# Grouped-query attention on one core: rounds of six jobs instead of five, and a new order of work in each sort of job

## The chip, the core and the metric

The kernel runs on one NeuronCore of one Trainium2 chip. The engines are TensorE (PE; its weight loads are shown apart as PEld), VectorE (DVE), ScalarE (ACT), GpSimd (POOL) and SyncE (SP, which here only issues DMAs). The metric is the device time of one execution in microseconds (us), and the times of several executions are given by their median.

## The reference

Attention with 8 batches, 512 positions, 32 query heads, 8 key heads and 64 numbers a head; four query heads share one key head. All in float32:

```python
    scale = 1.0 / np.sqrt(dim)
    K_expanded = np.repeat(K, heads_per_group, axis=2)      # V likewise
    ...
    scores = np.einsum('bhqd,bhkd->bhqk', Q, K_expanded) * scale
    weights = np.exp(scores - np.max(scores, axis=-1, keepdims=True))
    weights = weights / (np.sum(weights, axis=-1, keepdims=True) + 1e-10)
    output = np.einsum('bhqk,bhkd->bhqd', weights, V_expanded)
```

## The kernel before

The work is cut into 64 jobs. A job is one key head of one batch with its four query heads, that is two pairs of heads (i = 0 and 1), and for each pair 4 key chunks (kc) times 2 heads (m): 16 blocks of 128 keys by 512 queries. Two jobs are a unit u, whose result `o_sb` is stored at once; eight jobs are a batch. Scores are computed transposed (keys on partitions), so that the exponentials can serve as weights of the second matrix product.

For each job:

- PE multiplies keys and queries (`scores`, line 280). Two blocks fill a tile `s_ps` of two banks of PSUM; there are two such tiles.
- ACT takes the exponential of a tile and writes float16 into `pt` (`act_tile`, line 296). A full tile is called a wide tile here, a single block a half tile.
- Two or three of the blocks of pair 1 don't go to ACT. DVE and POOL compute their exponentials by the bits of a float16: DVE turns scores into an integer `u` (`exp_d`, line 306, from the tile `d_ps`, of which there is one), masks its mantissa `f` (`exp_d2`, line 320), POOL computes `g` and the product `w`, and DVE adds `u` and `w` into `pt` (`exp_d4`, line 346). A job with three such blocks is called wide (`WIDE`, line 41), one with two narrow. Where a wide job is followed by a narrow one, DVE also computes `g`, so that POOL has `w` alone.
- PE multiplies `pt` and V (`pv`, line 365; 32 steps a pair, in an order of blocks that `blocks` gives). V has a column of ones, so the sums of the weights come along. There is one tile `pv` of PSUM for this.
- DVE takes the reciprocal of the sums and multiplies (`norm`, line 402) into `o_sb`.
- PE transposes the queries of the job after the next into a bank of `d_ps` (`trans_q`, line 207), and DVE copies them out to `qt`.

All of it is one long program whose order is written out by hand; every engine runs its instructions in that order and waits where it has to. The jobs overlap by one: in the loop's pass j, scores and exponentials are job j's, while `pv`, `norm` and `exp_d4` are those of `last`, job j − 1. A tile of a pool can be written anew when its last reader is done, so `pv` of a pair waits for the multiplication in `norm` of the pair before.

In the kernel before, jobs 4 to 61 are wide unless j % 5 is 2: four wide and a narrow one, from job 3 on. ACT runs a wide job's seven instructions as four wide tiles, a half tile and two wide tiles; the half tile's scores lie in a bank of `d_ps` beside the transposed queries. The third block of job j + 1 is multiplied and converted in job j, in the same bank, after ACT has read the half tile:

```python
        bank = d_tile()
        beside = act_tile(j, 4, bank) if taken(j) > 2 else None
        ...
        if taken(j + 1) > 2:
            exp_d(j + 1, 2, taken(j + 1), bank[:, 1:2, :], copies[0])()
```

`LOADS`, `KEYS` and `CHECKS` say in which job K, Q and V are loaded (on POOL's queue, ahead of the job's other work on POOL), in which SP's queue transposes a batch's keys (four transposing DMAs and two copies, `dma_k`), and in which DVE checks a quarter of a batch's V (`check_v`) and the sums of 16 pairs (`check_sums`); these checks decide at the end whether a general path has to run.

Of the kernel before, what the change touches and what calls it, by code (L numbers as in the profile page):

```python
# [40 lines left out]
WIDE = lambda j: 4 <= j < 62 and j % 5 != 2  # L41
# [26 lines left out]
def fast_path(ctx, tc, Q, K, V, out, flag, ident):  # L68
# [28 lines left out]
    ok = const_pool.tile([128, SPB * 2 * SC], FP32, name="ok")  # L97
    okv = const_pool.tile([128, B * SC], FP32, name="okv")
    okall = const_pool.tile([128, 1], FP32, name="okall")
# [152 lines left out]
    def act_tiles(j):  # L252
# [8 lines left out]
    CHECKS = {  # L261
        (j, at): divmod(n, SC) for n, (j, at) in enumerate(
            [(j, 0) for j in (3, 4, 6, 7, 8, 11, 12, 16, 17, 21, 22, 23, 26, 27, 31, 32)]
            + [(j, 0) for j in (36, 37, 38, 41, 42, 46, 47, 48, 51, 52, 56, 57, 60, 61, 62)]
            + [(62, 1)]
        )
    }

    KEYS = dict(zip((4, 10, 16, 26, 36, 41, 50), range(1, B)))
# [26 lines left out]
    def act_tile(j, n, spare=None):  # L296
        group = act_tiles(j)[n]
        i, kc, lo = group[0]
        ps = s_pool.tile([128, 2, S], FP32, name="s_ps") if spare is None else spare
        for _, _, m in group:  # L300
            scores(j, ps[:, m, :], i, kc, m)
        return nc.scalar.activation(  # L302
            out=jobs[j]["pt"][:, i, kc, lo:, :], in_=ps[:, lo:, :], func=EXP, scale=scale
        )

    def exp_d(j, lo, hi, ps, other=None):
        st = jobs.setdefault(j, {})
        if "u" not in st:
            for name, dtype in (("u", I16), ("f", I16), ("g", BF16), ("w", BF16)):
                st[name] = dve_pool.tile([128, 3, S], dtype, name=name + "16")[:, 0:taken(j), :]  # L310
        for n in range(lo, hi):
            apart(scores(j, ps[:, n - lo, :], DPAIR, *divmod(d_block(j) + n, 2)), other)
        return lambda: nc.vector.tensor_scalar(  # L313
            out=st["u"][:, lo:hi, :], in0=ps[:, 0:hi - lo, :], scalar1=A_U, scalar2=B_U,
            op0=ALU.mult, op1=ALU.add,
        )

    def exp_d2(j, engine=None):  # L320
        st = jobs[j]
        by_bits = engine is None
        engine = engine or nc.gpsimd
        odd = j == NJOB - 2 or WIDE(j) and not WIDE(j + 1)
        nc.vector.tensor_single_scalar(  # L325
            out=st["f"], in_=st["u"], scalar=1023, op=ALU.bitwise_and
        )

        def factor():
            (nc.vector if odd else engine).tensor_scalar(  # L330
                out=st["g"], in0=st["f"], scalar1=-EXP_F1,
                scalar2=EXP_K * 2.0 ** (24 * by_bits), op0=ALU.add, op1=ALU.mult,
            )

        def product():
            engine.tensor_tensor(  # L336
                out=st["w"], in0=st["g"], in1=st["f"].bitcast(FP16) if by_bits else st["f"],
                op=ALU.mult,
            )
# [18 lines left out]
    def blocks(j, i):  # L358
        if j == NJOB - 1:
            kcs = (0, 1, 3, 2)  # L360
# [24 lines left out]
    def in_bounds(outs, inv, first):  # L385
        ops = ((1.0 / SUM_HI, ALU.is_ge), (1.0 / SUM_LO, ALU.is_le))
        for out_, in1, (bound, op) in zip(outs, (first, outs[0]), ops):
            nc.vector.scalar_tensor_tensor(
                out=out_, in0=inv, scalar=bound, in1=in1, op0=op, op1=ALU.mult
            )  # L390


    full = []

    def check_sums():
        while full:
            flat = invs.pop(full.pop()).rearrange("p s m qc -> p (s m qc)")
            in_bounds((ok, ok), flat, ok)
# [3 lines left out]
    def norm(j, i):  # L402
# [15 lines left out]
        if left == 1:  # L418
            last_rights(LAST_SUMS - 4 * SC, LAST_SUMS, nc.vector)
            last_check()  # L420
        h = g * HPG + 2 * i
# [12 lines left out]
        if left > NLAST and n == SPB - 1:  # L434
            full.append(k)

    def all_checks():
        assert not full and not invs
        vmax = const_pool.tile([128, 1], FP32, name="vmax")
        nc.vector.tensor_reduce(out=vmax, in_=okv, op=ALU.max, axis=AX.X)  # L440
        okmin = const_pool.tile([128, 1], FP32, name="okmin")
        nc.vector.tensor_reduce(out=okmin, in_=ok, op=ALU.min, axis=AX.X)
        nc.gpsimd.tensor_scalar(
            out=okall, in0=vmax, scalar1=V_HI, scalar2=okmin, op0=ALU.is_le, op1=ALU.mult
        )

    LIMITS = ((1.0 / SUM_HI, ALU.is_ge), (1.0 / SUM_LO, ALU.is_le))
    rights = [const_pool.tile([128, LAST_SUMS], BF16, name=f"right{n}") for n in range(2)]

    def last_rights(lo, hi, first=None):  # L450
        inv = inv_last.rearrange("p s m qc -> p (s m qc)")
        for engine, right, (bound, op) in zip((first or nc.gpsimd, nc.gpsimd), rights, LIMITS):
            engine.tensor_scalar(
                out=right[:, lo:hi], in0=inv[:, lo:hi],
                scalar1=bound, scalar2=okall, op0=op, op1=ALU.mult,
# [48 lines left out]
    nc.gpsimd.memset(ok, 1.0)  # L504
# [53 lines left out]
    exp_d(0, 0, 2, d_tile())()  # L558
# [11 lines left out]
    for j in range(1, NJOB - 1):  # L570
        last = j - 1
        u, g = divmod(j, 2)
        b, gp = divmod(u, GP)
        open_job(j)
# [9 lines left out]
        cut = (11, 19) if taken(j) < 3 else (4, 18) if taken(last) < 3 else (4, 16)  # L584
        act_tile(j, 0)
        if j == 1:
            piece(1, *first_k(1, 0, bank[:, 1, S // 2:]))
        exp_d(j, 0, 2, d_tile())()
        act_tile(j, 1)
        if j % 5 == 3:  # L590
            check_sums()
        if (j, 0) in CHECKS:
            check_v(*CHECKS[j, 0])
        pv(last, 0, 0, 16)
        act_tile(j, 2)
        pv(last, 0, 16, 32)
        norm(last, 0)
        act_tile(j, 3)

        reads = []  # L600
        bank = d_tile()
        beside = act_tile(j, 4, bank) if taken(j) > 2 else None

        ahead = (j + 1,) if j < 2 else (3, 4) if j == 2 else (j + 2,)
        for n, to in enumerate(ahead):
            if to < NJOB:
                reads.append(trans_q(to, bank[:, n, :], other=beside)[1])
        if j == 1:
            reads.append(first_k(1, 1, bank[:, 1, :])[1])
        exp_d4(last)  # L610
        rest = exp_d2(j)
        copies = [read() for read in reads]
        if rest:
            rest()
        if taken(j) == 2:
            act_tile(j, 4)
        pv(last, 1, 0, cut[0])
        act_tile(j, 5)
        if beside:
            pv(last, 1, *cut)  # L620
        if taken(j + 1) > 2:
            exp_d(j + 1, 2, taken(j + 1), bank[:, 1:2, :], copies[0])()
        if (j, 1) in CHECKS:
            check_v(*CHECKS[j, 1])
        if not beside:
            pv(last, 1, *cut)
        act_tile(j, 6)
        pv(last, 1, cut[1], 32)
        norm(last, 1)
# [5 lines left out]
    exp_d(j, 0, 2, d_tile())()  # L635
# [140 lines left out]
```

## Time and profile before

| | |
|---|---|
| runs, median (lowest to highest) | 404.34 us (404.28 to 404.49), 3 runs |
| profiled execution, its own time | 404.57 us |
| its span, first to last instruction | 402.8 us |
| granted TensorE clock, mean | 0.999 |
| HBM read, written | 50.33 MB, 33.55 MB |

A row of a timeline has the start in us from the span's start, the length, engine, line, operation, what is written from what, shapes and count; rows of equal instructions that follow each other are merged, and in square brackets stands the idle time before and what ended it. A row of groups has count, busy us, mean ns of one, idle us before it. A row of landings has the number of DMAs, their size and the median us from issue to landing.

### The profile page before, as it was taken

The page shows a single profiled execution, that of the slowest core. Times are in us where ns is not written, and L with a number is a line of the kernel's source. Part 1 is how long each engine was busy: PE and PEld are TensorE (multiplying, and loading weights), DVE is VectorE, ACT ScalarE, POOL GpSimd, SP SyncE. Part 2 cuts the span into 40 slices and gives each one's busy share as a digit, 9 for nine tenths or more (in the row PEclk, how much of TensorE's full clock was granted, in tenths as well). Part 3 has the DMA queues.
Part 4 walks back from the last instruction along what each step waited for, and adds up shares of the span by engine and source line. Part 5 has one row for each costly group of instructions (what it writes and reads, how often), then busy time and mean ns, then how long its engine had stood idle before and what let it go on. Part 6 is the DMA issues. An engine that isn't in the chain of part 4 may idle for free.

```text
span 402.8 us, 12997 instructions
## 1 busy us (share of the span) xinstructions
PE 375.8 (93%) x5670; PEld 228.0 (57%) x5670; DVE 366.4 (91%) x635; ACT 393.9 (98%) x454; POOL 286.8 (71%) x169
## 2 busy tenths in 40 slices
PE   7999999999999999999999999999999999999985
PEld 3565555555555555555555555555555555556554
DVE  4788998999999999999999999999999999999996
ACT  5999999999999999999999999999999999999995
POOL 9848577597587687687687686677776767765752
PEclk9999999999999999999999999999999999999999
DMA  9979999899999259999259999679369959222206
GB/s 145 163 190 182 91 288 225 164 211 237 184 214 206 107 88 247 192 239 182 107 84 226 168 227 197 208 109 252 110 170 202 175 169 128 107 106 106 88 34 201
DMA packets 82893, 67.73 MB, mean 168 GB/s; under 512 B 52752, under 2 KB 57872, under 8 KB 82832
## 3 DMA queue, kind: packets, MB, share of 16 engines
q0 software_dynamic: 45072, 24.91, 48.3%
q1 hardware_dynamic: 36688, 41.49, 36.6%
q8 instruction: 45, 0.74, 0.7%
q10 hardware_dynamic: 1072, 0.46, 0.4%
q14 instruction: 16, 0.13, 0.1%
HBM read 50.33 MB, written 33.55 MB: 208 GB/s over the span
## 4 chain that ended last, share of the span: by engine, by line
ACT 29%; PE 25%; POOL 24%; DVE 20%; issue 2%; ACTq 0%; DVEq 0%
ACT pt L302 28%; POOL w L336 16%; PE pv L377 12%; PE s_ps L284 9%; POOL g L330 8%; DVE pt L349 8%; DVE o_sb L422 4%; DVE f L325 4%; DVE qt L220 2%; PE d_ps L215 2%; DVE g L330 1%; DVE inv L417 1%; PE d_ps L284 1%; PE s_ps L510 1%; PE d_ps L377 0%
## 5 line engine op out<-in xcount | busy, mean ns | idle before, releaser
L302 ACT ACTIVATE pt<-s_ps 128x1024 f16<-128x1024 f32 x400 | 379.0, 1122 | 0.3 <-PE s_ps L284 0.2
L336 POOL TENSOR_TENSOR w<-g,f 128x1536 bf16<-128x1536 bf16 (+1 forms) x63 | 179.6, 2851 | 37.6 <-DVE g L330 33.4
L377 PEld LDWEIGHTS <-pt 128*128 128x128 f16 x4096 | 142.1, 98 | 81.2 <-issue 41.6
L377 PE MATMUL pv<-v,pt 128*128 128x65 bf16 x4032 | 177.8, 195 | 3.7 <-DVE o_sb L422 2.2
L284 PE MATMUL s_ps<-qt,kt 64*128 64x512 bf16 x746 | 152.3, 384 | 12.0 <-ACT pt L302 10.0
L330 POOL TENSOR_SCALAR g<-f 128x1536 bf16<-128x1536 int16 (+1 forms) x50 | 67.1, 1341 | 69.1 <-DVE f L325 69.0
L313 DVE TENSOR_SCALAR u<-d_ps 128x1024 int16<-128x1024 f32 (+1 forms) x111 | 109.9, 990 | 0.3
L284 PEld LDWEIGHTS <-kt 64*128 64x128 bf16 x960 | 50.2, 93 | 55.3 <-issue 31.5
L422 DVE TENSOR_TENSOR o_sb<-pv,inv 128x512 f32<-128x512 f32 x112 | 77.5, 692 | 3.9
L284 PE MATMUL d_ps<-qt,kt 64*128 64x512 bf16 x214 | 58.4, 376 | 3.5 <-ACT pt L302 0.3
L349 DVE TENSOR_TENSOR pt<-u,w 128x1536 uint16<-128x1536 int16 (+1 forms) x64 | 56.4, 882 | 2.3 <-POOL w L336 0.2
L220 DVE COPY qt<-d_ps 128x1024 bf16<-128x1024 bf16 x62 | 42.3, 684 | 0.0
L215 PEld LDWEIGHTS <-q_nat 128*128 128x128 bf16 x508 | 28.5, 98 | 23.8 <-issue 23.8
L417 DVE RECIPROCAL inv<-pv 128x8 f32<-128x8 f32 x112 | 23.1, 207 | 17.4 <-PE pv L377 16.0
L215 PE MATMUL d_ps<-ident,q_nat 128*128 128x128 bf16 x496 | 38.3, 220 | 0.0
L302 ACT ACTIVATE pt<-d_ps 128x512 f16<-128x512 f32 x47 | 34.0, 724 | 0.0
L325 DVE TENSOR_SCALAR f<-u 128x1536 int16<-128x1536 int16 (+1 forms) x64 | 33.3, 521 | 0.0
L238 DVE TENSOR_REDUCE okv<-v 128x1 f32<-128x512 bf16 x32 | 21.6, 676 | 0.0
L142 POOL DMA_DIRECT2D q_nat<-in_Q_dram x19 | 15.2, 801 | 0.1
L284 PE MATMUL s_ps<-qt,kt_first 64*128 64x512 bf16 x56 | 11.1, 396 | 1.9 <-ACT pt L302 1.5
L127 POOL DMA_DIRECT2D v<-in_V_dram x7 | 12.3, 1753 | 0.0
L422 DVE TENSOR_TENSOR o_sb<-pv,inv_last 128x512 f32<-128x512 f32 x14 | 9.7, 692 | 0.5
(61 smaller groups left out, 62.7 us busy)
## 6 DMA issues: line engine op xcount, KB each, us to landing
out_dram<-o_sb SPq DMA_DIRECT2D x31, 1024.0 KB, 6.1
q_nat<-in_Q_dram POOLq DMA_DIRECT2D x14, 1024.0 KB, 12.4
k_nat<-in_K_dram POOLq DMA_DIRECT2D x7, 512.0 KB, 7.5
v<-in_V_dram POOLq DMA_DIRECT2D x7, 512.0 KB, 13.6
kt<-kt SPq DMA_DIRECT2D x14, 256.0 KB, 4.0
q_nat<-in_Q_dram POOLq DMA_DIRECT2D x3, 512.0 KB, 7.5
out_dram<-o_sb SPq DMA_DIRECT2D x3, 256.0 KB, 2.4
kt<-k_nat SPq DMA_TRANSPOSE x32, 5.9
```

The source lines that it names most:

```text
L215: nc.tensor.transpose(ps[:, i, sc, :], qn[u // 2][:, sc, h:h + 2, :], ident),
L220: return done, lambda: apart(nc.vector.tensor_copy(out=qt[u][:, g, lo:hi, :], in_=ps[:, lo:hi, :, :].rearrange("p i sc c -> p i (sc c)")), ...
L284: return nc.tensor.matmul(ps, keys[64 * m:64 * m + 64, g if u == 0 else g ^ m, kc * 128:(kc + 1) * 128], qt[u][64 * m:64 * m + 64, g, i, : ...
L302: return nc.scalar.activation(out=jobs[j]["pt"][:, i, kc, lo:, :], in_=ps[:, lo:, :], func=EXP, scale=scale)
L313: return lambda: nc.vector.tensor_scalar(out=st["u"][:, lo:hi, :], in0=ps[:, 0:hi - lo, :], scalar1=A_U, scalar2=B_U, op0=ALU.mult, op1=AL ...
L325: nc.vector.tensor_single_scalar(out=st["f"], in_=st["u"], scalar=1023, op=ALU.bitwise_and)
L330: (nc.vector if odd else engine).tensor_scalar(out=st["g"], in0=st["f"], scalar1=-EXP_F1, scalar2=EXP_K * 2.0 ** (24 * by_bits), op0=ALU.a ...
L336: engine.tensor_tensor(out=st["w"], in0=st["g"], in1=st["f"].bitcast(FP16) if by_bits else st["f"], op=ALU.mult,)
L349: nc.vector.tensor_tensor(out=st["pt"][:, DPAIR, :, :, :].rearrange("p kc m q -> p (kc m) q")[:, d_block(j):d_block(j) + n, :].bitcast(U16 ...
L377: nc.tensor.matmul(st["pv"][i][:, m, qc, :], st["pt"][:, i, kc, m, qc * 128:(qc + 1) * 128], vt[b % 2][:, kc, 2 * gp + g, :], start=(n < 2 ...
L417: nc.vector.reciprocal(out=inv, in_=sums[:, :, :, D:D + 1])
L422: nc.vector.tensor_tensor(out=osb[u][:, :, h:h + 2, :].rearrange("p qc m d -> p m qc d"), in0=sums[:, :, :, 0:D], in1=inv[:, :, :, None].t ...
```

## The change

- `WIDE` becomes 3 <= j < 62 with j % 6 other than 2: ten rounds of five wide jobs and a narrow one, jobs 3 to 62. `ALONE` names the last wide job of a round and job 62, where DVE computes `g`.
- The third block of a wide job is multiplied and converted in that job (`odd_tile`): its scores go into bank 0 of a tile `d_ps` and those of ACT's half tile into bank 1, one pair of matrix products; DVE reads one bank, ACT the other, and the transposed queries then go into bank 0.
- The loop's body has four orders: jobs 1 and 2 as before, narrow jobs, wide jobs, and the last wide job of a round, which also multiplies the first tile of the job after it. The cuts of `pv` between them are new, and so is the order of blocks in `blocks`: key chunk 1's block of ACT comes before VectorE's three.
- On DVE, the third block's conversion now stands ahead of `exp_d4`; in the last wide job, `g` stands between the reciprocal and the multiplication of pair 1.
- `check_sums` takes minimum, maximum and sum of a chunk with three reductions, and `all_checks` reduces these at the end; before, two operations a chunk kept a running product. The jobs of loads, key transposes and checks are new.

```diff
-WIDE = lambda j: 4 <= j < 62 and j % 5 != 2
+WIDE = lambda j: 3 <= j < 62 and j % 6 != 2
+ALONE = lambda j: j == 62 or WIDE(j) and not WIDE(j + 1)
...
+    CHECKS = [n + i for n in (4, 10, 16, 22, 28, 40, 46, 52) for i in range(SC)]
+    SUMS = dict(zip((14, 20, 26, 38, 44, 50, 62), range(B - 1)))
-    KEYS = dict(zip((4, 10, 16, 26, 36, 41, 50), range(1, B)))
+    KEYS = dict(zip((4, 10, 17, 28, 33, 41, 52), range(1, B)))
...
-    in_jobs(load_k, 1, [3, 8, 12, 23, 32, 38, 48])
-    in_jobs(load_q, 2, [3, 7, 8, 12, 17, 22, 23, 27, 32, 37, 38, 42, 47, 48])
-    in_jobs(load_v, 1, [4, 13, 18, 28, 33, 43, 53])
+    in_jobs(load_k, 1, [3, 8, 15, 22, 30, 39, 46])
+    in_jobs(load_q, 2, [3, 5, 9, 12, 16, 21, 23, 28, 33, 35, 40, 45, 47, 52])
+    in_jobs(load_v, 1, [7, 13, 19, 25, 37, 43, 49])
...
+    def odd_tile(j, ps):
+        (i, kc, m), = act_tiles(j)[4]
+        scores(j, ps[:, 0, :], i, kc, 0)
+        scores(j, ps[:, m, :], i, kc, m)
+        st = jobs[j]
+        left = nc.scalar.activation(
+            out=st["pt"][:, i, kc, m:, :], in_=ps[:, m:, :], func=EXP, scale=scale
+        )
+        apart(to_bits(st["u"][:, 2:3, :], ps[:, 0:1, :]), left)
+        return left
...
-            kcs = (2, 3, 1, 0)
-        return [(kc, m, qc) for kc in kcs for m in range(2) for qc in range(SC)]
+            kms = [(2, 0), (2, 1), (3, 0), (3, 1), (1, 1), (1, 0), (0, 0), (0, 1)]
+        return [(kc, m, qc) for kc, m in kms for qc in range(SC)]
...
+    FOUND = (ALU.min, ALU.max, ALU.add)
+    def check_sums(k):
+        flat = invs.pop(k).rearrange("p s m qc -> p (s m qc)")
+        for n, op in enumerate(FOUND):
+            nc.vector.tensor_reduce(out=found[:, n, k:k + 1], in_=flat, op=op, axis=AX.X)
...
+        elif taken(j) < 3:
+            act_tile(j, 1)
+            checks()
+            exp_d(j, d_tile())
+            act_tile(j, 2)
+            pv(last, 0, 0, 12)
+            act_tile(j, 3)
+            pv(last, 0, 12, 32)
+            norm(last, 0)
+            act_tile(j, 4)
+            reads = transposes(d_tile()) if j + 2 < NJOB else []
+            exp_d4(last)
+            for read in reads:
+                read()
+            rest = exp_d2(j)
+            if rest:
+                rest()
+            act_tile(j, 5)
+            pv(last, 1, 0, 16)
+            act_tile(j, 6)
+            pv(last, 1, 16, 32)
+            norm(last, 1)
+        elif not ALONE(j):
+            after = taken(last) < 3
+            act_tile(j, 0)
+            exp_d(j, d_tile())
+            act_tile(j, 1)
+            checks()
+            pv(last, 0, 0, 16)
+            act_tile(j, 2)
+            pv(last, 0, 16, 32)
+            norm(last, 0)
+            act_tile(j, 3)
+            bank = d_tile()
+            beside = odd_tile(j, bank)
+            act_tile(j, 5)
+            cut = 14 if after else 19
+            pv(last, 1, 0, cut)
+            if after:
+                act_tile(j, 6)
+            reads = transposes(bank, beside)
+            if not after:
+                act_tile(j, 6)
+            exp_d4(last)
+            exp_d2(j)
+            for read in reads:
+                read()
+            pv(last, 1, cut, 32)
+            norm(last, 1)
+        else:
+            act_tile(j, 0)
+            act_tile(j, 1)
+            exp_d(j, d_tile())
+            checks()
+            act_tile(j, 2)
+            pv(last, 0, 0, 16)
+            act_tile(j, 3)
+            bank = d_tile()
+            beside = odd_tile(j, bank)
+            pv(last, 0, 16, 32)
+            norm(last, 0)
+            act_tile(j, 5)
+            reads = transposes(bank, beside)
+            act_tile(j, 6)
+            pv(last, 1, 0, 20)
+            exp_d4(last)
+            rest = exp_d2(j)
+            for read in reads:
+                read()
+            open_job(j + 1)
+            act_tile(j + 1, 0)
+            pv(last, 1, 20, 32)
+            norm(last, 1, rest)
```

More of the change, by code (lines that the diff above doesn't have):

```diff
@@ L383, in pv, with norm @@
             )
[L385 to L398, printed above, removed]
+    FOUND = (ALU.min, ALU.max, ALU.add)
[3 more added lines that the diff above has]
+            nc.vector.tensor_reduce(out=found[:, n, k:k + 1], in_=flat, op=op, axis=AX.X)
     inv_last = const_pool.tile([128, NLAST, 2, SC], FP32, name="inv_last")
-    def norm(j, i):
+    def norm(j, i, between=None):
         st = jobs[j]
@@ L433, in norm @@
             store(u, 0, 2 * HPG)
-        if left > NLAST and n == SPB - 1:
-            full.append(k)
+    LIMITS = ((1.0 / SUM_HI, ALU.is_ge), (1.0 / SUM_LO, ALU.is_le))
     def all_checks():
[L438 to L447, printed above, removed]
+        assert not invs
+        for n, op in enumerate(FOUND):
+            nc.vector.tensor_reduce(out=seen_all[:, n:n + 1], in_=found[:, n, :], op=op, axis=AX.X)
+        nc.vector.tensor_reduce(out=seen_all[:, 3:4], in_=okv, op=ALU.max, axis=AX.X)
+        right = 1.0
+        for n, (bound, op) in enumerate((*LIMITS, (1.0e30, ALU.is_le), (V_HI, ALU.is_le))):
+            nc.gpsimd.tensor_scalar(
+                out=okall[:, n:n + 1], in0=seen_all[:, n:n + 1],
+                scalar1=bound, scalar2=right, op0=op, op1=ALU.mult,
+            )
+            right = okall[:, n:n + 1]
     rights = [const_pool.tile([128, LAST_SUMS], BF16, name=f"right{n}") for n in range(2)]
@@ L600, in fast_path @@
[L600 to L614, printed above, removed]
@@ L615, in fast_path, with transposes @@
-        if taken(j) == 2:
-            act_tile(j, 4)
[L617 to L629, printed above, removed]
+        def transposes(bank, beside=None):
+            ahead = (j + 1,) if j < 2 else (3, 4) if j == 2 else (j + 2,)
+            return [
+                trans_q(to, bank[:, n, :], other=beside)[1]
+                for n, to in enumerate(ahead) if to < NJOB
+            ]
```

100 lines of the change are left out of this document (55 added, 45 removed).

## The prediction

> **What bounds the kernel now.** I read the page's table of engines first, then ScalarE's timeline, then the sums over the stretch that the change rewrites, then the timeline of the other engines inside single jobs, and last the landings of the V loads.
>
> ```profile
> PE 375.8 (93%) x5670; PEld 228.0 (57%) x5670; DVE 366.4 (91%) x635; ACT 393.9 (98%) x454; POOL 286.8 (71%) x169
> 25.71 10.22 ACT L302 ACTIVATE pt<-s_ps 128x1024 f16<-128x1024 f32 x11
> 151.88 5.66 ACT L302 ACTIVATE pt<-s_ps 128x1024 f16<-128x1024 f32 x6
> 157.31 0.72 ACT L302 ACTIVATE pt<-d_ps 128x512 f16<-128x512 f32 x1
> 157.78 5.75 ACT L302 ACTIVATE pt<-s_ps 128x1024 f16<-128x1024 f32 x6
> 391.17 6.60 ACT L302 ACTIVATE pt<-s_ps 128x1024 f16<-128x1024 f32 x7
> 25.71:391.17 365.46, 346.23 (x5272) 210.11 (x5272) 342.75 (x586) 365.33 (x421) 263.44 (x136) 1.00 0.84 169
> ```
>
> ACT is busy 98% of the span, but a busy ACT isn't an ACT at its fastest: successive exponentials overlap, so the spacing of starts counts. At 151.88 six wide tiles take 157.31 − 151.88 = 5.43, or 0.905 each, and a half tile 157.78 − 157.31 = 0.47. A job with three blocks on VectorE (a wide job: six wide tiles, one half tile) can thus take 6 × 0.905 + 0.47 = 5.90, a job with two (a narrow one: seven wide tiles) 6.34. Job 3 begins at 25.71 and job 63 at 391.17, 365.46 for the sixty jobs that the change rewrites; 47 of them are wide and 13 narrow, 47 × 5.90 + 13 × 6.34 = 359.7. So ACT, though never idle, loses 5.8 there to tiles whose scores come late. The last row (columns: length, then PE, its weight loads, DVE, ACT, POOL) says that DVE is busy 342.75 of it, 94%: close behind.
>
> **The change, part by part.** Of the sixty jobs 50 become wide, five in a row and then a narrow one. The half tiles stay one to a wide job, so ACT's own floor falls to 50 × 5.90 + 10 × 6.34 = 358.4, or 35.84 a round. Could the others keep up, the gain were 7.1. What speaks against it is a loop that ACT isn't in:
>
> ```profile
> 184.63 0.65 PE L377 MATMUL pv<-v,pt 128*128 128x65 bf16 x16
> 185.23 0.39 PE L284 MATMUL s_ps<-qt,kt 64*128 64x512 bf16 x2
> 185.55 0.65 PE L377 MATMUL pv<-v,pt 128*128 128x65 bf16 x16
> 186.24 0.21 DVE L417 RECIPROCAL inv<-pv 128x8 f32<-128x8 f32 x1 [0.53 <-PE pv L377]
> 186.49 0.69 DVE L422 TENSOR_TENSOR o_sb<-pv,inv 128x512 f32<-128x512 f32 x1
> 187.09 0.95 DVE L349 TENSOR_TENSOR pt<-u,w 128x1536 uint16<-128x1536 int16 x1
> 187.96 0.55 DVE L325 TENSOR_SCALAR f<-u 128x1536 int16<-128x1536 int16 x1
> 188.43 0.69 DVE L220 COPY qt<-d_ps 128x1024 bf16<-128x1024 bf16 x1
> 188.60 1.47 POOL L330 TENSOR_SCALAR g<-f 128x1536 bf16<-128x1536 int16 x1 [1.58 <-DVE f L325]
> 189.03 0.68 DVE L313 TENSOR_SCALAR u<-d_ps 128x512 int16<-128x512 f32 x1
> 190.16 3.10 POOL L336 TENSOR_TENSOR w<-g,f 128x1536 bf16<-128x1536 bf16 x1
> 193.29 0.96 DVE L349 TENSOR_TENSOR pt<-u,w 128x1536 uint16<-128x1536 int16 x1
> ...
> 174.97 0.95 DVE L349 TENSOR_TENSOR pt<-u,w 128x1536 uint16<-128x1536 int16 x1
> 175.84 0.42 DVE L325 TENSOR_SCALAR f<-u 128x1024 int16<-128x1024 int16 x1
> 176.17 0.69 DVE L220 COPY qt<-d_ps 128x1024 bf16<-128x1024 bf16 x1
> ...
> 181.12 0.68 DVE L349 TENSOR_TENSOR pt<-u,w 128x1024 uint16<-128x1024 int16 x1
> 181.72 0.55 DVE L325 TENSOR_SCALAR f<-u 128x1536 int16<-128x1536 int16 x1
> ...
> 201.44 0.55 DVE L330 TENSOR_SCALAR g<-f 128x1536 bf16<-128x1536 int16 x1
> ```
>
> On DVE the addition that ends job j−1's exponentials (`exp_d4`) stands ahead of `f` of job j; `f` feeds `g` and `w` on POOL, and `w` the next addition. Neither engine can shorten that loop: 187.09 to 193.29, 6.20 (addition 0.87 to `f`, 0.55, 0.09, 1.47, 0.09, 3.10, 0.03). It is longer than a wide job's 5.90, so in a run of wide jobs the addition slips 0.30 a job against ACT, and the last wide and the narrow job must win it back. Before, runs are four long; now five, with a new order around them. I add up the loop over a new round, along what waits for what in the new order:
>
> - narrow's addition to that of the job after it (0.60 to `f`, by 181.12 and 181.72, in place of 0.87): 5.93;
> - three wide steps: 18.60;
> - the last wide job, whose `g` now stands on DVE behind the query copy and the reciprocal: 0.87 + 0.47 + 0.60 (188.43 to 189.03) + some 0.17 for the reciprocal (its row: 0.21 long) + `g` 0.55 + 0.10 to POOL + 3.10 + 0.03 = 5.89;
> - the narrow job to the first wide one. There the path leaves POOL: addition 0.87, copy 0.60, `f` 0.33 (175.84 to 176.17), reciprocal 0.25, product 0.69, then 0.05 until PE may write the single `pv` buffer, 1.61 for its two batches of 16 with a pair of scores between (184.63 to 186.24), reciprocal 0.25, product 0.60, and the third block's conversion 0.60, which the change has put ahead of the addition: 5.85.
>
> Together 36.27 a round. That is 0.43 over ACT's 35.84, so ACT will wait 0.4 to 0.5 in each round, and ten rounds take 362.7 against 365.46: 2.8 less. The wait surfaces as late scores: PE stands in order, and a late addition holds `pv` of pair 1, a late product `pv` of pair 0, and the next score pairs are queued behind either. Going through the windows by these rows, the late tile is e2 of the fourth wide job (some 0.3), and a little in the narrow one.
>
> A rule of the Trainium skill speaks against lengthening the runs: GPSIMD Engine Reference, Specifications, has GpSimd's SBUF interfaces shared with VectorE, contending with VectorE's two-input and two-port instructions, of which the change adds some. The trace must show it in `w`:
>
> ```profile
> L336 POOL TENSOR_TENSOR w<-g,f x63: 2122/3095/3107, 12.0 to 390.0; 128x1536 bf16<-128x1536 bf16 x47, 128x1024 bf16<-128x1024 bf16 x16
> L336 POOL TENSOR_TENSOR w<-g,f 128x1536 bf16<-128x1536 bf16 x47 | 145.6, 3098 | 34.2 <-DVE g L330 31.3
> ```
>
> The 47 long ones have a mean of 3098 and a maximum of 3107 ns beside a DVE that is busy 94%; I take 3.10. The page's rule isn't seen in that row, and is a rival below.
>
> **Loads.** K and Q loads fall in POOL's gap before `g` (1.58 at 188.60) or in wider ones. V loads, moved to the last wide job, stand between `w` of the job before and a `w` that waits for DVE's `g`: 0.87 + 0.47 + 0.60 + 0.17 + 0.55 + 0.10 = 2.76, and they issue in 1.75:
>
> ```profile
> 32.99 1.75 POOL L127 DMA_DIRECT2D v<-in_V_dram  x1
> v<-in_V_dram POOLq DMA_DIRECT2D x7, 512.0 KB, 13.6
> DMA to landing us min/median/max: 5.2/9.0/17.8
> v<-in_V_dram POOLq DMA_DIRECT2D x1, 512.0 KB, 9.1
> v<-in_V_dram POOLq DMA_DIRECT2D x1, 512.0 KB, 16.5
> ```
>
> So POOL hides the issue. The landing is another matter for batch 1. Its V goes from job 4 (issued at 32.99, landed after 16.5: the last row, for that one load) to job 7, behind `w` of job 6, and `pv` of job 8, at the head of job 9, needs it. From there to that `pv` the loop leaves the last wide job's 5.89 and, of the next step, 0.87 + 0.60 + 0.33 + 0.25 + 0.69 + 0.05 = 2.79, plus the 0.03 behind `w`: 8.7. An undisturbed load takes 9.1 (fourth row: the last V load, issued at 331.73); with the store of the unit before beside it I take 9.2, a wait of 0.5, from none up to 7.8 at 16.5. The other V loads have three jobs' time (over 15 us) until the check that reads them, with landings of 13.6 in the median (second row).
> The Trainium skill's fit (DMA: Bandwidth & Descriptors, Anatomy of one DMA) is 2.0 us plus bytes by 436 per ns, for 512 KB an estimate of 3.2; by it the wait vanishes and the sum falls by 0.5. The rows of this trace are close to three times that and more, so it isn't used.
>
> The key transposes on SP start later for batches 3, 4, 5 and 7, but at least four jobs, 24 us, ahead of their use. The slowest in the trace runs from 33.98 to the landing of its last copy, 49.0 + 0.5 + 4.3: 20 us. So it costs nothing; if traffic makes it a fifth slower, each further us costs one.
>
> ```profile
> 33.98 6.15 SPq L193 DMA_TRANSPOSE kt<-k_nat  x4
> 49.00 1.11 SPq L198 DMA_DIRECT2D kt<-kt  x2
> kt<-kt SPq DMA_DIRECT2D x2, 256.0 KB, 4.3
> ...
> L238 DVE TENSOR_REDUCE okv<-v 128x1 f32<-128x512 bf16 x32 | 21.6, 676 | 0.0
> ```
>
> **Small parts.** V checks (0.68 each, the last row) lie in the second to fifth wide jobs, where DVE waits for `w` anyway: free while that cover lasts. If it goes, what exceeds DVE's idle 6% (0.37 of a job) counts, 0.3 for each. `check_sums` goes from two operations on 128 numbers a chunk to three, in narrow jobs, where nothing of the loop above stands behind them but a conversion that is early. At the end `all_checks` has two reductions more, and the addition stands later in job 62: 0.2, my estimate, by the 0.25 and 0.05 of the small steps above. Jobs 0 to 2 keep their order: nothing.
>
> **Sum.** The profiled execution took 404.57 (span 402.8); of it the sixty jobs 365.46. New: 362.7 + 0.5 + 0.2 = 363.4, so 402.5. The median of the runs, 404.34, lies 0.23 lower: 402.3. Every link of the loop is a lower bound, since each must be gone through and I gave none a delay; 0.05 a round for that puts the forecast at 402.8.
>
> **Rivals.**
> *ACT alone sets the pace.* The loop has slack that I don't see (a link counted that nobody waits for). Then 358.4 + 0.7 replaces 365.46: 398.2 less 0.23, 398.0. Against it: 6.20 is seen in the trace as a bound already. 0.05.
> *The narrow job loses more.* Its first `pv` waits for the product that now stands behind `g`: 0.87 + 0.47 + 0.60 + 0.17 + 0.47 + 0.69 + 0.05 = 3.32 after the addition of the last wide job, and the narrow job's order leaves its third and fourth tiles some 0.1 of room. Should 0.2 to 0.4 a round be lost there and passed round the loop, the time is 404.4 to 406.4. 0.16.
> *Batch 1's V is late, and it ends slower.* Landing after 16.5 as before costs 7.8 in place of 0.5: 410.1. For it: with other traffic the median of the seven landings was 13.6. Against: the Q load ahead of it goes two jobs earlier. It decides from a landing of 10.8 (no gain left); 0.13.
> *VectorE slows GpSimd.* Five `w` stand in a round's loop. 5% on each is 0.78 a round, 410.6; from 1% (0.16 a round) the gain is gone. The constant 3.10 speaks against it. 0.04. (This is the skill's rule on the shared interface.)
>
> **How the numbers follow.** The forecast's own case gets 0.62: 401.0 (the estimated links 0.1 shorter, V in time) to 404.2. Under 0.2%, 0.8 us, a measurement of this kernel can hardly tell from no change. Faster, below 403.5: 0.55 of the forecast's case and ACT's 0.05, 0.60. Same: 0.07 of it, 0.09 of the narrow job's, 0.01 of V's, 0.17. Slower: 0.07, 0.12 and 0.04, 0.23. The range, 401.0 to 406.0, leaves out ACT's case, V's beyond a landing of some 12.5, and GpSimd's.
>
> **What would show it.** Additions 6.20 apart through the wide jobs, with DVE idle until `w`; rounds near 36.3 by ACT's half tiles; 50 half tiles; an idle PE before `pv` in job 9 until V lands, 9 to 10 after its issue; `w` still 3.10. Wrong: rounds of 35.9, or over 36.5; a `w` above 3.13; V landing beyond 10.8.

## The result and the profile after

The kernel after takes 406.06 us (median of 6 runs, 405.64 to 406.47), the kernel before beside it 404.40 (6 runs, 404.28 to 405.45): a ratio of 1.0037, 95% interval 1.0024 to 1.0050. It is slower by 0.4%, where 402.8 (401.0 to 406.0) and faster was forecast. The profiled execution of after took 405.98, with a span of 404.2 and a granted clock of 0.999.

From the page of after, busy time by engine and two groups:

```profile
PE 362.4 (90%) x5670; PEld 223.9 (55%) x5670; DVE 369.6 (91%) x645; ACT 394.1 (97%) x454; POOL 294.8 (73%) x173
L334 DVE TENSOR_SCALAR f<-u 128x1536 int16<-128x1536 int16 (+1 forms) x64 | 37.6, 588 | 0.0
L131 POOL DMA_DIRECT2D v<-in_V_dram x7 | 12.4, 1765 | 0.0
```

The groups of after by shape, `w` alone:

```profile
L345 POOL TENSOR_TENSOR w<-g,f 128x1536 bf16<-128x1536 bf16 x50 | 154.7, 3094 | 22.7 <-DVE g L339 19.4
```

And the sums over jobs 3 to 62 of after (stretch, its length, then PE, its weight loads, DVE, ACT, POOL):

```profile
25.67:392.45 366.78, 333.63 (x5272) 206.39 (x5272) 346.02 (x594) 365.44 (x422) 269.07 (x138) 1.00 0.83 168
```

The sixty jobs take 366.78 in place of 365.46, 1.32 more. The profiled executions differ by 1.41 (405.98 and 404.57); the tail behind job 62 makes up the remaining 0.1. `w` keeps its 3.09 for 50 instructions, so POOL's loop should hold. The odd row is `f`, with a mean of 588 ns over all 64. Its masks of three blocks alone, in the groups of before and of after by shape:

```profile
L325 DVE TENSOR_SCALAR f<-u 128x1536 int16<-128x1536 int16 x47 | 26.0, 554 | 0.0
...
L334 DVE TENSOR_SCALAR f<-u 128x1536 int16<-128x1536 int16 x50 | 31.8, 636 | 0.0
```

The loop can be read off VectorE's additions (timeline of DVE in after, the rows of `exp_d4` alone, from the last wide job of one round to the narrow job of the next):

```profile
200.88 0.96 DVE L358 TENSOR_TENSOR pt<-u,w 128x1536 uint16<-128x1536 int16 x1
206.66 0.96 DVE L358 TENSOR_TENSOR pt<-u,w 128x1536 uint16<-128x1536 int16 x1
212.61 0.68 DVE L358 TENSOR_TENSOR pt<-u,w 128x1024 uint16<-128x1024 int16 x1
218.62 0.95 DVE L358 TENSOR_TENSOR pt<-u,w 128x1536 uint16<-128x1536 int16 x1
224.81 0.96 DVE L358 TENSOR_TENSOR pt<-u,w 128x1536 uint16<-128x1536 int16 x1
231.02 0.96 DVE L358 TENSOR_TENSOR pt<-u,w 128x1536 uint16<-128x1536 int16 x1
237.21 0.96 DVE L358 TENSOR_TENSOR pt<-u,w 128x1536 uint16<-128x1536 int16 x1
243.60 0.96 DVE L358 TENSOR_TENSOR pt<-u,w 128x1536 uint16<-128x1536 int16 x1
```

The three wide steps behind 218.62 are 6.19, 6.21 and 6.19, as forecast. From the last wide job's addition to the narrow job's it is 206.66 − 200.88 = 5.78 in job 32, and 243.60 − 237.21 = 6.39 in job 38. Job 31 has no V load; job 37 has one. Seven of the ten rounds have one.

ACT's half tiles show the same in the length of a round. The first two rows below are the first half tiles of two successive rounds around job 31, the last two around job 49, which has a V load:

```profile
176.31 0.63 ACT L310 ACTIVATE pt<-d_ps 128x512 f16<-128x512 f32 x1
212.52 0.80 ACT L310 ACTIVATE pt<-d_ps 128x512 f16<-128x512 f32 x1
...
286.49 0.63 ACT L310 ACTIVATE pt<-d_ps 128x512 f16<-128x512 f32 x1
323.25 0.63 ACT L310 ACTIVATE pt<-d_ps 128x512 f16<-128x512 f32 x1
```

36.21 without a V load, within 0.1 of the forecast of 36.27, and 36.76 with one.

Below, what a job loses is its length, by the starts of ACT's exponentials, over the prediction's 5.90 for a wide and 6.34 for a narrow job. What the load does is in the timelines of job 43 (DVE, POOL and PE of after):

```profile
274.31 0.96 DVE L358 TENSOR_TENSOR pt<-u,w 128x1536 uint16<-128x1536 int16 x1
275.18 1.16 DVE L334 TENSOR_SCALAR f<-u 128x1536 int16<-128x1536 int16 x1
276.26 0.67 DVE L224 COPY qt<-d_ps 128x1024 bf16<-128x1024 bf16 x1
276.97 0.50 DVE L339 TENSOR_SCALAR g<-f 128x1536 bf16<-128x1536 int16 x1
277.39 0.68 DVE L425 TENSOR_TENSOR o_sb<-pv,inv 128x512 f32<-128x512 f32 x1
...
274.22 1.76 POOL L131 DMA_DIRECT2D v<-in_V_dram  x1
277.56 3.09 POOL L345 TENSOR_TENSOR w<-g,f 128x1536 bf16<-128x1536 bf16 x1 [1.58 <-DVE g L339]
...
278.13 0.54 PE L386 MATMUL pv<-v,pt 128*128 128x65 bf16 x12 [0.53 <-DVE o_sb L425]
```

POOL issues the load at 274.22 for 1.76, in its gap before `w`, as the prediction had it; it even idles 1.58 behind it. But beside the issue VectorE's mask `f` takes 1.16, where it takes 0.55 otherwise. Behind it the copy, `g`, the output product and `w` come 0.6 later against the addition than in job 31. PE's first `pv` of the narrow job waits for that product (the single tile `pv`) until 278.13, the score pairs queued behind it wait as well, and ACT loses 0.52 in the narrow job, job 44. Behind the other loads it loses 0.52 or 0.53, but 0.19 in job 8 and 0.79 in job 38; the narrow jobs of the three rounds without a load lose nothing.

### The profile page after: what moved, and what is told of

It is laid out like the page before. It is cut to its first block, busy times and chain, and to the rows that moved or that the text cites. A ratio compares the mean times of both kernels' runs of the same rounds, so it can differ in the third digit from the quotient of the medians.

```text
span 404.2 us, 13018 instructions
## 1 busy us (share of the span) xinstructions
PE 362.4 (90%) x5670; PEld 223.9 (55%) x5670; DVE 369.6 (91%) x645; ACT 394.1 (97%) x454; POOL 294.8 (73%) x173
## 4 chain that ended last, share of the span: by engine, by line
POOL 28%; PE 27%; DVE 20%; ACT 19%; issue 3%; DMA 2%; ACTq 0%; POOLq 0%; DVEq 0%
ACT pt L300 19%; POOL w L345 17%; PE pv L386 13%; PE s_ps L282 10%; POOL g L339 8%; DVE pt L358 8%; DVE f L334 5%; PE d_ps L219 3%; DVE o_sb L425 3%; DMA q_nat<-in_Q_dram 2%; DVE u L317 2%; DVE qt L224 1%; POOL v L129 1%; DVE inv L418 1%; DVE g L339 1%
## 5 line engine op out<-in xcount | busy, mean ns | idle before, releaser
L345 POOL TENSOR_TENSOR w<-g,f 128x1536 bf16<-128x1536 bf16 (+1 forms) x63 | 182.3, 2894 | 25.6 <-DVE g L339 21.3
L386 PEld LDWEIGHTS <-pt 128*128 128x128 f16 x4096 | 140.5, 98 | 69.2 <-DVE o_sb L425 35.6
L386 PE MATMUL pv<-v,pt 128*128 128x65 bf16 x4032 | 170.1, 195 | 7.1 <-DVE o_sb L425 5.5
L282 PE MATMUL s_ps<-qt,kt 64*128 64x512 bf16 x742 | 145.1, 384 | 21.1 <-ACT pt L300 17.7
L339 POOL TENSOR_SCALAR g<-f 128x1536 bf16<-128x1536 int16 (+1 forms) x52 | 71.1, 1368 | 76.3 <-DVE f L334 60.1
L317 DVE TENSOR_SCALAR u<-d_ps 128x1024 int16<-128x1024 f32 (+1 forms) x114 | 111.9, 981 | 2.1 <-PE d_ps L282 1.8
L358 DVE TENSOR_TENSOR pt<-u,w 128x1536 uint16<-128x1536 int16 (+1 forms) x64 | 57.4, 897 | 3.1
L282 PE MATMUL d_ps<-qt,kt 64*128 64x512 bf16 x218 | 42.1, 377 | 4.9 <-DVE qt L224 4.3
L334 DVE TENSOR_SCALAR f<-u 128x1536 int16<-128x1536 int16 (+1 forms) x64 | 37.6, 588 | 0.0
```

The source lines that it names most:

```text
L282: return nc.tensor.matmul(ps, keys[64 * m:64 * m + 64, g if u == 0 else g ^ m, kc * 128:(kc + 1) * 128], qt[u][64 * m:64 * m + 64, g, i, : ...
L317: return nc.vector.tensor_scalar(out=out, in0=in_, scalar1=A_U, scalar2=B_U, op0=ALU.mult, op1=ALU.add)
L334: nc.vector.tensor_single_scalar(out=st["f"], in_=st["u"], scalar=1023, op=ALU.bitwise_and)
L339: (nc.vector if odd else engine).tensor_scalar(out=st["g"], in0=st["f"], scalar1=-EXP_F1, scalar2=EXP_K * 2.0 ** (24 * by_bits), op0=ALU.a ...
L345: engine.tensor_tensor(out=st["w"], in0=st["g"], in1=st["f"].bitcast(FP16) if by_bits else st["f"], op=ALU.mult,)
L358: nc.vector.tensor_tensor(out=st["pt"][:, DPAIR, :, :, :].rearrange("p kc m q -> p (kc m) q")[:, d_block(j):d_block(j) + n, :].bitcast(U16 ...
```

## The experiments

Theory A: a V load's issue on GpSimd stretches VectorE's `f`, and that lateness costs the round. Rivals: the narrow job is late for another reason (the sums' three reductions, `g` ahead of the output product), or the transfer itself is what costs. The letters in what follows are those of each experiment's own expectation, which stands ahead of its result.

### V in halves

```diff
+    def load_v_half(b, half):
...
-    in_jobs(load_v, 1, [7, 13, 19, 25, 37, 43, 49])
+    for half, at in enumerate(([6, 13, 19, 25, 37, 43, 49], [7, 14, 20, 26, 38, 44, 50])):
+        for b, j in enumerate(at, 1):
+            LOADS.setdefault(j, []).append((load_v_half, b, half))
```

> The changed kernel with each V load cut in two halves: one issued on GpSimd at the start of the last wide job (for batch 1 of the job before it), the other at the start of the job after that. An issue of half the length (about 0.9 us) ends while VectorE is still at the addition or the query copy, so it no longer lies beside f. Theory A (the issue of a whole V load, 1.76 us, lies beside f in the last wide job, stretches it from 0.55 to 1.16 us and with it the loop of addition, f, g, w): no f over 0.65 us, the narrow job's addition 4.1 instead of 4.7 after its first tile in every round, its loss 0.0 instead of 0.5, rounds of 36.2 to 36.4, 402.5 us (402.1 to 403.2). Theory B (the round is lost to the reductions of the sums, which lie in the same narrow jobs, or to the order of the narrow job itself): the narrow jobs lose 0.5 as before and the time stays at 406.

403.43 us (403.05 to 403.96, 11 runs), ratio to before 0.9977 (0.9968 to 0.9986): faster than both kernels, though 0.2 above the top of theory A's range. The issue of a half took 1.2 us, not the 0.9 expected, and the longest `f` is nearly back to normal. The row of all `f` (minimum, median, maximum ns), of this kernel:

```profile
L343 DVE TENSOR_SCALAR f<-u x64: 416/553/635, 10.0 to 391.9; 128x1536 int16<-128x1536 int16 x50, 128x1024 int16<-128x1024 int16 x14
```

The narrow jobs lose 0.03 or less in place of 0.53, but for job 38 (0.28 in place of 0.79). This fits A, but moves bytes as well as issue.

### The order before, with V in the last wide job

```diff
-    in_jobs(load_v, 1, [4, 13, 18, 28, 33, 43, 53])
+    in_jobs(load_v, 1, [4, 11, 21, 26, 36, 46, 51])
```

> The kernel before with six of its seven V loads moved to the last wide job of a round, where VectorE computes g, so that their issue lies beside f as in the changed kernel. Theory A: f in those six jobs takes 1.0 to 1.2 us instead of 0.55, but the loop of addition, f, g and w has over 1 us to spare in a round of five (28.9 against 30.4), so the time stays within 0.8 us of 404.4. If f stays at 0.55 us there, the stretch isn't made by the V issue but by something of the new order. If each costs 0.5 (3 us in all), the loop has no room in the kernel before either.

408.03 us (one run), against 404.4 for before: 3.6 for six moved loads. Timelines of DVE and POOL of this kernel in one such job:

```profile
140.47 1.15 DVE L325 TENSOR_SCALAR f<-u 128x1536 int16<-128x1536 int16 x1
...
139.50 1.76 POOL L127 DMA_DIRECT2D v<-in_V_dram  x1
```

So the stretch needs none of the change's new orders; only the place of the load counts. The room that I had allowed the old order wasn't there: the six narrow jobs behind the moved loads lose 0.56 to 0.59 more than in the kernel before, 3.4 together, which is nearly all of the 3.6.

### The sums one job later

```diff
-    SUMS = dict(zip((14, 20, 26, 38, 44, 50, 62), range(B - 1)))
+    SUMS = dict(zip((15, 21, 27, 39, 45, 51, 62), range(B - 1)))
```

> The changed kernel with six of its seven check_sums (three reductions of 128 numbers) moved from the narrow job to the first wide job of the next round. Theory A: f still takes 1.16 us in the V rounds and the narrow job still loses 0.4 to 0.55; 405.6 to 406.4 us. Theory B (the reductions hold up the conversion of the narrow job and through it the transposes and the next score pairs): the narrow job's loss falls below 0.2, 403 us.

406.55 us (one run). The reductions are out of the narrow job, which loses 0.53 all the same; `f` beside the load (timeline of DVE of this kernel) is as long as ever:

```profile
275.57 1.15 DVE L334 TENSOR_SCALAR f<-u 128x1536 int16<-128x1536 int16 x1
```

The sums aren't it.

### The mask behind the copy

This is the sharpest test: V stays whole and in its place, and in the last wide job two instructions of VectorE change places.

```diff
             exp_d4(last)
-            rest = exp_d2(j)
             for read in reads:
                 read()
+            rest = exp_d2(j)
```

> The changed kernel with V loaded whole in the last wide job as it is, but in that job VectorE takes the copy of the transposed Q ahead of the mask f, so that f begins 0.6 us later beside the issue of 1.76 us. Theory A (only f is stretched by the issue on GpSimd, the copy from PSUM is not, and the half microsecond a round is that stretch handed on through the output product, the single pv bank and TensorE): f is beside the issue for 0.2 us and takes 0.55 to 0.75 us instead of 1.16, the narrow job's addition comes back from 4.69 to 4.1 to 4.3 us after its first tile, it loses 0.0 to 0.15 us instead of 0.54: 402.7 to 403.7 us. Rival B (anything on VectorE in that window pays, or the transfer itself does): the copy or f takes the half microsecond, 405.5 to 406.5 us.

403.41 us (403.24 to 404.19, 11 runs), ratio to before 0.9976 (0.9967 to 0.9985): 2.65 us less than the kernel after. Timelines of POOL and DVE of this kernel, job 43:

```profile
272.30 1.76 POOL L131 DMA_DIRECT2D v<-in_V_dram  x1
...
273.28 0.68 DVE L224 COPY qt<-d_ps 128x1024 bf16<-128x1024 bf16 x1
273.88 0.55 DVE L334 TENSOR_SCALAR f<-u 128x1536 int16<-128x1536 int16 x1
```

The row of all its `f`, as above:

```profile
L334 DVE TENSOR_SCALAR f<-u x64: 414/551/572, 10.0 to 391.5; 128x1536 int16<-128x1536 int16 x50, 128x1024 int16<-128x1024 int16 x14
```

The copy, beside the issue for all of its length, keeps its 0.68; `f`, which now begins 0.19 before the issue ends, keeps its 0.55. The narrow jobs lose 0.03 or less, but for job 38 (0.27). The transfer is the same as before the swap, so rival B falls. Nor does the new order gain by itself: in the three rounds without a V load the swap gains nothing (36.35, 36.61 and 36.33, against 36.22, 36.49 and 36.34 in after), while the seven with one fall from 36.71 to 37.14 to 36.29 to 36.64. So A is shown: the loss of after against before comes from this one pairing.

### V whole, in the narrow job

```diff
-    in_jobs(load_v, 1, [7, 13, 19, 25, 37, 43, 49])
+    in_jobs(load_v, 1, [8, 14, 20, 26, 38, 44, 50])
```

> The changed kernel with each V load whole, but issued one job later, in the narrow job. GpSimd has then no product beside it for VectorE's next addition until the first wide job, whose addition came 0.6 to 0.9 us after its w. Theory A (only VectorE's mask f loses beside the issue; in the narrow job it is smaller, 0.42 us for 128x1024, and starts 1.5 us after the issue of 1.76 us began): f is beside the issue for 0.3 us only, so VectorE loses under 0.3 us a round and the narrow jobs lose 0.0 to 0.1 us as with V in halves: 402.8 to 404.0 us. Rival B (an issue of 1.76 us costs half a microsecond wherever it stands, by GpSimd's lost time rather than VectorE's): the first wide job's addition waits for w instead, 405.5 to 406.5 us.

421.84 us (421.15 to 426.07, 4 runs), ratio 1.0459 (1.0410 to 1.0508): far from what either theory expected. Batch 1's V is needed in job 9, and the edit left it one job. The landings of two loads of this kernel, the first issued at 61.16 (batch 1), the second at 114.25:

```profile
v<-in_V_dram POOLq DMA_DIRECT2D x1, 512.0 KB, 18.0
v<-in_V_dram POOLq DMA_DIRECT2D x1, 512.0 KB, 7.7
```

PE at the head of job 9 (timeline of PE of this kernel):

```profile
79.31 1.04 PE L386 MATMUL pv<-v,pt 128*128 128x65 bf16 x16 [15.69 <-DMA v<-in_V_dram]
```

PE waited 15.69, and job 9 lost 17.4. In job 8, `f` began 0.74 before the end of this load's issue and took 0.96 in place of 0.42. The six other loads answer the question: there `f` of the narrow job starts in the issue's last 0.2 us and takes 0.42 to 0.43, and the narrow jobs lose 0.02 or less but for job 38 (0.27, much as in the kernels with V in halves and with the mask behind the copy). In these rounds this is A again; an issue of 1.76 costs next to nothing where it isn't beside `f`. The time as a whole doesn't show it: the profiled 421.96 less the 17.4 is 404.6, still above A's range. Job 3 begins 0.9 later than in the kernel with the mask behind the copy, and jobs 40 and 41 lose 0.5 more than there; neither is explained.

### `g` of the third wide job on VectorE too

On the kernel with V in halves, to take 1.1 us out of POOL's loop.

```diff
+        near = odd or WIDE(j) and j % 6 == 5
-            (nc.vector if odd else engine).tensor_scalar(
+            (nc.vector if near else engine).tensor_scalar(
```

> The kernel with the halved V loads, and in the third wide job of each round VectorE computes g as well, so GpSimd has w alone there. That takes 1.08 us out of the loop in each round (a step of 0.87 + 0.47 + 0.55 + 0.10 + 3.10 + 0.03 = 5.12 instead of 6.20) and adds 0.47 us of VectorE work. Theory A with the loop as the bound of the round (36.27): the loop falls to 35.2, ScalarE's own 35.84 is next: rounds of 35.9 to 36.1 and 398.8 to 400.8 us. If ScalarE or TensorE, not the loop, set the rounds of the halved kernel, nothing changes against it (402.5); if VectorE does, it is slower by up to 4.7 us.

408.19 us (408.11 to 408.67, 4 runs), ratio 1.0097 (1.0082 to 1.0113): 4.8 slower than without the edit, so theory A's 398.8 to 400.8 is refuted. The next step of the additions grows from 6.20 to 6.60, and `w` is done 1.4 before the addition. I took this for VectorE's load and tested that by leaving out the checks of V:

```diff
+    nc.vector.memset(okv, 0.0)
...
-            for n, at in enumerate(CHECKS):
-                if at == j:
-                    check_v(*divmod(n, SC))
```

> The kernel with V in halves and g of the third wide job on VectorE, with the checks of V (32 reductions of 0.68 us on VectorE) left out: its output is the same, the check of V's range is not made. Theory A (with g moved, VectorE's own instructions in their order set the step of 6.60 us, not GpSimd): the step falls by about a check to 6.0 to 6.2 us, the fourth wide job loses 0.35 us or less instead of 0.82, the time is 402.0 to 403.5 us. Rival B (the step of 6.60 comes from the chain f, g, w, addition or from TensorE, not from VectorE's load): the step stays over 6.45, and the time above 406.5 us.

407.88 us (one run); the step is still 6.60, so this experiment's theory A falls and rival B stands. Timelines of DVE and PE of this kernel without checks:

```profile
299.54 0.96 DVE L369 TENSOR_TENSOR pt<-u,w 128x1536 uint16<-128x1536 int16 x1
300.42 0.55 DVE L345 TENSOR_SCALAR f<-u 128x1536 int16<-128x1536 int16 x1
301.00 0.56 DVE L350 TENSOR_SCALAR g<-f 128x1536 bf16<-128x1536 int16 x1
301.48 0.68 DVE L232 COPY qt<-d_ps 128x1024 bf16<-128x1024 bf16 x1
302.31 0.69 DVE L436 TENSOR_TENSOR o_sb<-pv,inv 128x512 f32<-128x512 f32 x1
304.69 0.21 DVE L429 RECIPROCAL inv<-pv 128x8 f32<-128x8 f32 x1 [0.55 <-PE pv L397]
306.14 0.95 DVE L369 TENSOR_TENSOR pt<-u,w 128x1536 uint16<-128x1536 int16 x1
307.00 0.55 DVE L345 TENSOR_SCALAR f<-u 128x1536 int16<-128x1536 int16 x1
307.47 0.68 DVE L232 COPY qt<-d_ps 128x1024 bf16<-128x1024 bf16 x1
...
302.22 0.39 PE L292 MATMUL d_ps<-qt,kt 64*128 64x512 bf16 x2 [0.80 <-DVE qt L232]
303.06 0.67 PE L397 MATMUL pv<-v,pt 128*128 128x65 bf16 x16 [0.24 <-DVE o_sb L436]
303.98 0.67 PE L397 MATMUL pv<-v,pt 128*128 128x65 bf16 x16
```

There is a second loop, through PE: addition, `f`, here `g`, copy, reciprocal, output product, then the free tile `pv` lets PE write the next `pv` (303.06 to 304.65), and VectorE, idle for 0.55 before 304.69, takes reciprocal, product and conversion up to the next addition: 306.14 − 299.54 = 6.60. With `g` the copy starts 1.06 behind `f` (300.42 to 301.48), without it 0.47 (307.00 to 307.47): `g` adds 0.59. Without it the loop is some 6.0, just below POOL's 6.20. So anything that adds over 0.2 to VectorE ahead of its output product sets the step; `g` did, and the stretched `f` delays the same product.

### Rounds of five with the new orders, V in halves

```diff
-WIDE = lambda j: 3 <= j < 62 and j % 6 != 2
+WIDE = lambda j: 3 <= j < 62 and j % 5 != 2
```

(With V in halves as above, and the jobs of loads, keys, checks and sums moved to suit.)

> The orders of the changed kernel and V in halves, but rounds of five jobs (narrow jobs 7, 12, ..., 62; loads, keys and checks placed anew; wide jobs 48 instead of 50). Theory A (a round is the sum of its wide steps at 6.20 us set by GpSimd's loop, and its narrow steps of 5.9, as rounds without a V load showed): a round of five is 5.93 + 2 x 6.20 + 5.89 + 5.85 = 30.07 us, 6.014 a job against 6.045, so twelve rounds take 360.8 where ten of six took 362.7: 1.9 us less than the kernel with V in halves, 401.5 us (400.8 to 402.3). Rival B (the narrow job, which comes 12 times instead of 10, costs more than the loop gives back, since VectorE is late by its end): 403.4 us or more. Rival C (ScalarE, whose least work a round of five is 5.90 x 4 + 6.34 = 29.94, loses over 0.3 a round elsewhere): between the two, and the addition would no longer start 0.03 us after w.

403.70 us (403.61 to 404.47, 11 runs), ratio 0.9988 (0.9979 to 0.9997), no better than rounds of six. The additions of one round (timeline of DVE of this kernel):

```profile
181.85 0.68 DVE L367 TENSOR_TENSOR pt<-u,w 128x1024 uint16<-128x1024 int16 x1
187.82 0.95 DVE L367 TENSOR_TENSOR pt<-u,w 128x1536 uint16<-128x1536 int16 x1
194.03 0.96 DVE L367 TENSOR_TENSOR pt<-u,w 128x1536 uint16<-128x1536 int16 x1
200.34 0.95 DVE L367 TENSOR_TENSOR pt<-u,w 128x1536 uint16<-128x1536 int16 x1
206.25 0.95 DVE L367 TENSOR_TENSOR pt<-u,w 128x1536 uint16<-128x1536 int16 x1
```

Steps of 5.97, 6.21, 6.31 and 5.91. The step into the last wide job is 6.31, not 6.20 (there the addition stands 0.15 behind `w`), and the narrow jobs lose about 0.15 each in the median. Theory A's 401.5 is refuted; rival B has the time right (403.4 or more), and C's sign, an addition no longer 0.03 behind `w`, is there too.

### The fifth wide job's first tile earlier, V in halves

```diff
+            if j % 6 == 0:
+                open_job(j + 1)
+                act_tile(j + 1, 0)
             pv(last, 1, cut, 32)
```

(The last wide job then leaves its own first tile out.)

> The kernel with V in halves; in the fourth wide job ScalarE's first tile of the fifth is put ahead of the last thirteen blocks of the second product with V, as the last wide job has it for the narrow one. The fourth wide job, which lost 0.31 us a round, should lose none. Theory A (the round is the sum of GpSimd's loop steps, 36.27 us, whichever job shows the loss): the additions keep their steps of 6.20 us, so the fifth wide and the narrow job are that much later in themselves and lose it there: 403.0 to 404.0 us, no change from 403.43. Rival B (the narrow job's own slack, where the first wide job's addition comes 0.6 us after w, takes the delay up, so that ScalarE's least work of 35.84 us sets the round): 0.3 us a round less, 400.2 to 401.2 us.

403.06 us (402.46 to 403.30, 5 runs), ratio 0.9964 (0.9950 to 0.9978). The fourth wide job loses 0.22 in place of 0.31, the narrow one mostly 0.08 to 0.15 in place of 0.03 or less; the round from job 15 to job 21 is 36.37 in both. Theory A holds: the loop sets the round, and the orders only choose which job shows the loss. What is gained, 0.5 over the sixty jobs, lies nearly all in the rounds of jobs 6 and 54, which lose more than others (36.25 and 36.35 here, 36.48 and 36.59 with V in halves). The interval overlaps that of V in halves; all of these three versions (halves, mask behind the copy, earlier tile) beat the kernel before by 0.2 to 0.4%, and the kernel after by more.

## Why the prediction was wrong, step by step

- *POOL's loop.* Right. Steps of 6.20 in the wide jobs, addition 0.03 behind `w`, `w` at 3.09. Where no V issue is beside `f`, the rows of the kernel with the mask behind the copy give a round of 5.83 (forecast 5.89) + 5.87 to 5.91 (5.85) + 6.01 (5.93) + 18.60 = 36.31 to 36.35, against 36.27. The 6.01 is the term that was too small by 0.08: there the addition stands 0.12 behind `w`, held by the loop through PE, which I had counted for one step only.
- *"So POOL hides the issue."* This is the step that failed. The gap was there (the issue and 1.58 of idle time fit) and POOL lost nothing. But I asked only whether the issuing engine had time, not what the issue does to VectorE, whose `f` runs beside it. In the trace of before no V issue stood beside a wide `f`, and I took its absence from the rows for a price of nothing, with no upper bound. There was a hint: two masks of two blocks beside the issue of a Q load took 0.48 and 0.50 there, one beside that of a first V load 0.44, the others 0.42. Seven stretched masks added some 0.6 to one step of the loop each; the first wide jobs win back a part, and 2.65 in all remain (406.06 − 403.41). That is more than the forecast's 1.5 of gain, and turns its sign.
- *The sum otherwise.* Without that pair the kernel takes 403.41, 1.1 above the 402.3 of the sum and 0.6 above the forecast. Its sixty jobs take 364.18 where 362.7 was forecast: ten times 0.08, and three rounds that are 0.15 to 0.3 longer, with jobs 6, 38 and 54 losing more than the same sort of job elsewhere. The 0.5 for batch 1's V, which didn't come, hid a part of it. Jobs 6, 38 and 54 lose more in the kernel before too (0.21, 0.32 and 0.42 there, where most jobs at their places in a round lose 0.02 to 0.05, 0.02 to 0.05 and 0.09 to 0.14), so the new rounds aren't the reason; the cause is open.
- *Batch 1's V.* It landed 8.2 after its issue, and job 9 didn't wait; 0.5 was counted. The rival's mechanism is real, as the load one job later showed with a wait of 15.7, but the landing of after wasn't near its threshold of 10.8. The long landings, 16.5 in before and 18.0 there, went with other DMAs in flight: a K load, a Q load and the four key transposes of a batch in both. The batch 1 load of after had two stores beside it and, in its last 2 us, a K load. Which of these DMAs makes a landing long wasn't tested.
- *The narrow job loses more.* The place was right (its first `pv` waits for the output product) and the measured median lies in its range (404.4 to 406.4), but that is luck, for its reason was wrong: with `g` ahead of the product and no V load the narrow job loses nothing.
- *VectorE slows GpSimd.* No: `w` has a mean of 3094 beside a VectorE busy 94% of that stretch. The engines do get in each other's way, but at GpSimd's DMA issue, and VectorE pays.
- *Small parts.* No engine waits for a transposed key or a loaded V in the waits of after. The checks cost nothing in the one step, with `g` moved, where they were taken away and looked at. The tail grew by 0.1 in place of 0.2.
- *What would show it wrong.* A round over 36.5 was named, and the rounds with a V load are 36.7 to 37.1. Of the signs that it is right, additions 6.20 apart, 50 half tiles and `w` at 3.10 came; PE's wait for V in job 9 didn't.

## What to carry to other kernels

A DMA that GpSimd issues isn't hidden because GpSimd has a gap: look at what VectorE runs beside the issue, and keep a mask such as `f` out of that window, by its place in the order if nothing else. When an engine's loop is the bound, look for the next loop behind it (here 6.0 behind 6.2), since it turns a small delay on another engine into time. And where the trace of before never shows a pairing that the change makes, give its price a bound from both sides; nothing seen isn't nothing paid.

## What the runs showed of the hardware

The length of `f` beside a V issue isn't random. In after, each of the seven masks of three blocks ends 0.36 us behind the issue (the first: issue 53.75 to 55.52, `f` 54.88 to 55.88), whether it had begun 0.63 or 0.81 before the issue's end. With V in halves, where seven overlaps are 0.25 to 0.28, it is 0.36 again; the two-block mask of the kernel with V in the narrow job (0.74 of overlap) ends 0.22 behind its issue. A mask at half speed would end nearer to the issue's end the earlier it had begun. So the length fits a mask that stands still until the issue is over, and an overlap of up to 0.2 us is free. VectorE's addition (two inputs from SBUF) and its copy out of PSUM run through the same issue with their usual 0.96 and 0.68, and the issue keeps its 1.76.

One early pair in after goes the other way (timelines of POOL and DVE of after):

```profile
9.45 1.00 POOL L129 DMA_DIRECT2D v<-in_V_dram  x1
9.61 0.43 DVE L334 TENSOR_SCALAR f<-u 128x1024 int16<-128x1024 int16 x1
```

Here `f` lies within the issue of one of the first V loads and keeps its 0.43, and the issue takes 1.00. In the kernel with the fifth wide job's first tile earlier the same pair lies likewise, with 1.04; in the others, with no mask in its first 0.4 us, that issue takes 0.83 to 0.88. So the issue can be the one that pays; what decides it isn't shown.

The Trainium skill says this in SBUF — State Buffer, Who interferes with whom: GpSimd and VectorE share one pair of ports under an exclusive lock, `tensor_scalar` can take the pair while `tensor_tensor` doesn't take the part that writing descriptors is inferred to need, and the second to come is blocked in full, not slowed. The traces fit this with the numbers above, but for the early pair, where by the starts in the trace the mask came second and yet wasn't held. Its warning is written for the DMA that waits for VectorE; here VectorE waited for the DMA's issue. The prediction weighed the same sharing from GPSIMD Engine Reference, Specifications, against `w` alone, and so looked for it in the wrong instruction.
